# Branch A's attention with values as weights: the output comes out turned, and the division follows it

## The chip, the cores and the metric

The kernel runs on one core of a Trainium2 chip. The metric is the device time of one execution in microseconds (us). A core has a matrix engine (TensorE; PE for its matmuls and PEld for its weight loads in the profile), VectorE (DVE), ScalarE (ACT), GpSimd (POOL) and SyncE (SP), which issues most DMA transfers. Matmul results land in PSUM, in eight banks of 128 partitions by 512 f32; everything else works in SBUF.

## The reference

One layer of a bidirectional encoder, applied to a sample of 1024 tokens and a prompt of 256 tokens, 1024 channels wide, all in f32:

```python
h = _rmsnorm(x, g_mix)
z = h @ w_in                     # queries, keys, values of branches A and B, two gates
o_a, _ = _banded_attention(qa, ka, va, A_WINDOW, 1, rel_bias[:, :A_HEADS], sink)
o_b = _dilated_mixture(qb, kb, vb, rel_bias[:, A_HEADS:])
merged = gates[:, :, 0] * (o_a.reshape(b, S, A_Q) @ w_branch_a) + gates[:, :, 1] * (o_b @ w_branch_b)
x = x + merged @ w_out
h = _rmsnorm(x, g_mlp)
return x + jnp.square(jax.nn.relu(h @ w_up)) @ w_down
```

A final RMS norm follows. The change is in branch A: 8 query heads of 64 channels on 2 key and value heads, each query seeing the keys up to 128 tokens away, with a learned sink per head:

```python
p = jnp.exp(logits - m[..., None])
denom = jnp.sum(p, axis=-1) + jnp.exp(sink_r - m)
o = jnp.einsum('bngrqk,bnkgd->bnqgrd', p, vb)
o = o / denom[..., None]
```

## The kernel before

The 1280 tokens are ten tiles of 128 (tiles 0 to 7 are the sample, 8 and 9 the prompt). The program goes through stages: norm and values, the projections (with branch B's attention beside the last of them), branch A's attention, the gated branch outputs, the output projection, and the MLP. Most large products are made of three matmuls: each f32 operand is split into a high part (`hi`, a rounded copy made by ScalarE) and a low part (`lo`, the rest, subtracted by VectorE), and `mm3` (line 192) or `six` (line 351) multiplies low by high, high by low and high by high. Scores take two matmuls (lines 1071 and 1072). Probabilities and values are multiplied as plain f32, which the profile shows as two load and matmul passes for each matmul.

Branch A's attention runs head pair by head pair (`u`, 4 of them, two heads each) and tile by tile. A query tile sees its own key block of 128 and its neighbours: three blocks, or two at the ends of sample and prompt (tiles 0, 7, 8, 9). For one unit (head pair and tile), `scores` fills a bank for each head and VectorE adds the bias and takes the maximum; `exponential` is ScalarE's, and puts the row sums into `l_a`; `transposes` turns the probabilities on TensorE, and ScalarE (the first four blocks) and VectorE (the rest) move them to `pt`, whose slot `2 * b + h` holds block b of head h with keys on the partitions and queries in columns. `values_of` multiplies them into the one bank with tag "pv", VectorE copies the result to `o` (line 1111), and GpSimd writes it to the scratch tensor `scr_o[t]` (line 1112), a 128-column stripe for each head pair. The order on every engine is written out by hand here (a manual schedule): each turn of the loop handles two units, and between their steps it puts pieces of `logits`, the matmuls of five gate columns, and of `merge`, branch B's mixture, whose tiles `turn_merged` and `low_b` later turn and split.

After the last unit, `sums_a` adds the sink's share to `l_a` and takes the reciprocal. Then `load_o` (SyncE) brings back all heads of a tile, `divide` multiplies by the reciprocal sums on VectorE (line 1237), `turn_a` transposes the tile on TensorE (line 1246) and ScalarE writes its high part, and `low_a` makes the low part (line 1258). They run beside the 48 gated products ("jobs"): in a job TensorE multiplies a branch output of up to 512 tokens with 128 output columns, and VectorE multiplies the bank with the gate (lines 1385 and 1387) and adds for branch A (line 1388). The dictionary `side` says ahead of which job which step is issued; `load_gate` asks for a gate six jobs ahead (line 1332) and `open_gate` applies the sigmoid three jobs ahead (line 1337). The manual schedule ends before this loop; from there on a planner orders the instructions, in program order where it sees no reason against it, by costs it assumes.

Tiles of 4 KB for each partition come from one pool of 33 slots (`slot`). PSUM's banks are three "mm", two "sc", two "pt" and one "pv".

Of the kernel before, what the change touches and what calls it, by code (L numbers as in the profile page):

```python
# [13 lines left out]
ALU = mybir.AluOpType  # L14

P = 128
# [6 lines left out]
HD = 64  # L23
AH = 8
# [26 lines left out]
HALVES = (slice(0, HD), slice(HD, P))  # L51
# [46 lines left out]
def encoder_kernel(  # L98
# [5 lines left out]
    nc = tc.nc  # L104
# [22 lines left out]
    def slot(name, shape=(P, D), dt=F32):  # L127
        return slots.tile(list(shape), dt, name=name, tag="m", bufs=N_M)
# [7 lines left out]
    def bank(tag, name=None):  # L136
        return psum.tile([P, 512], F32, name=name or tag, tag=tag, bufs={"mm": 3, "sc": 2, "pt": 2, "pv": 1}[tag])
# [108 lines left out]
    ident = const.tile([P, P], F32, name="ident")  # L246
# [8 lines left out]
    l_a = const.tile([P, AH, NT], F32, name="l_a")  # L255
# [22 lines left out]
    scr_o = [dram.tile([P, AH * HD], F32, name=f"scr_o{t}") for t in range(NT)]  # L278
# [362 lines left out]
    with ExitStack() as pre:  # L641
# [166 lines left out]
        for t in range(2, NT):  # L808
# [13 lines left out]
            ps = bank("mm", "v")  # L822
# [18 lines left out]
        for t in (4, 5, 6, 7, 8, 9, 0, 1, 2, 3):  # L841
            ps = bank("mm", "v")
# [6 lines left out]
    if True:  # L849
# [177 lines left out]
        b, p = iter(()), parts0  # L1027
        att_b = iter(())
        for first, last, name in ((0, MIXED, "pairs"), (MIXED, len(PAIRS), "mixed")):
            with tc.tile_pool(name=name, bufs=1) as now[0]:  # L1030
                if first:
                    att_b = attention_b(stage)
                for j in range(first, last):
# [4 lines left out]
                    b, p = pair(b, p, PAIRS[j], PAIRS[j + 1] if j + 1 < len(PAIRS) else None, hooks, tick, first)  # L1038
# [10 lines left out]
    if True:  # L1049
# [7 lines left out]
        for t in range(NT):  # L1057
            s0, m = (0, 8) if t < 8 else (8, 2)
            lo, hi = max(t - 1, s0), min(t + 1, s0 + m - 1)
# [39 lines left out]
        def values_of(u, t):  # L1099
            lo, W, _ = tiles[t]  # L1100
            pt = live.pop((u, t))
            v, rest = units[u][0]["v"]
            pv = bank("pv")
            for h in range(2):
                for b in range(W // P):
                    k = lo + b
                    src = v[:, k, HALVES[u // 2]] if k < 8 else rest[:, k - 8, HALVES[u // 2]]
                    nc.tensor.matmul(pv[:, HD * h : HD * h + HD], pt[:, 2 * b + h, :], src,  # L1108
                                     start=b == 0, stop=b == W // P - 1)
            o = a3("o", (P, P), 3)  # L1110
            nc.vector.tensor_copy(o, pv[:, :P])
            nc.gpsimd.dma_start(scr_o[t][:, P * u : P * u + P], o)
# [88 lines left out]
    if True:  # L1201
        ob_hi, ob_lo = Wide("obhi", 2, F32R, ()), Wide("oblo", 2, F32R, ())
        o_hi, o_lo = Wide("ohi", 4, F32R, ()), Wide("olo", 4, F32R, ())
# [24 lines left out]
        rows_o = {}  # L1228

        def load_o(t):  # L1230
            rows_o[t] = slot("o", (P, AH, HD))
            nc.sync.dma_start(rows_o[t], scr_o[t].rearrange("p (h d) -> p h d", h=AH))

        def divide(t):

            o = rows_o[t]
            nc.vector.tensor_tensor(o, o, l_a[:, :, t].unsqueeze(2).to_broadcast([P, AH, HD]), op=ALU.mult)

        def turn_a(t):
            if t in (0, 4, 8):  # L1240
                o_hi.block(t // 4)
                o_lo.block(t // 4)
            o = rows_o.pop(t)
            ps = bank("pt")
            for k in range(4):
                nc.tensor.transpose(ps[:, P * k : P * k + P],
                                    o[:, 2 * k : 2 * k + 2, :].rearrange("p h d -> p (h d)"), ident)
            p3 = ps.rearrange("p (k q) -> p k q", k=4)
            per = o_hi.per(P * t)
            parts = [(o_hi.at(k, P * t, P, per), o_lo.at(k, P * t, P, per), p3[:, k : k + per, :])  # L1250
                     for k in range(0, 4, per)]
            banks_t["a", t] = parts
            for hi, _, src in parts:
                nc.scalar.activation(hi, src, AF.Copy)
# [14 lines left out]
        for j in range(0, n + 2, 2):  # L1269
# [31 lines left out]
            if j < n and order[j][1] == 0 and order[j][0] < 3:  # L1301
                u = order[j][0] + 1
# [40 lines left out]
        load_gate(3)  # L1343
        load_o(3)
        for i in range(4):
            divide(i)
            if i < 3:
                open_gate(i)
            next(fill)
        run(fill)  # L1350
        load_gate(4)
        load_gate(5)
        last.close()
        side = {0: [(turn_a, 0)], 1: [(low_a, 0), (turn_a, 1)], 2: [(low_a, 1), (turn_merged, 4)],
                3: [(low_b, 4), (turn_a, 2)], 4: [(low_a, 2), (turn_a, 3)], 5: [(low_a, 3), (turn_merged, 5)],
                6: [(low_b, 5), (turn_merged, 6)], 7: [(low_b, 6), (turn_merged, 7)], 8: [(low_b, 7), (divide, 4)],
                9: [(turn_a, 4), (divide, 5)], 10: [(low_a, 4), (turn_a, 5)], 11: [(low_a, 5), (divide, 6)],
                13: [(turn_a, 6)], 14: [(low_a, 6), (divide, 7)], 15: [(turn_a, 7)], 16: [(low_a, 7)],
                17: [(turn_merged, 8)], 18: [(low_b, 8), (turn_merged, 9)], 19: [(low_b, 9), (divide, 8)],
                20: [(turn_a, 8)], 21: [(low_a, 8), (divide, 9)], 22: [(turn_a, 9)], 23: [(low_a, 9)]}  # L1360
        for i, (x, b, c) in enumerate(jobs):
            t0, n = BLOCKS[b]
            load_gate(i + 6)
# [11 lines left out]
            hi, lo = w_bs[c // 4] if x == "b" else w_as[c // 2]  # L1375
            per, src = (4, (ob_hi, ob_lo)) if x == "b" else (2, (o_hi, o_lo))
            cols = slice(P * (c % per), P * (c % per) + P)
            ps = bank("mm")
# [76 lines left out]
    with ExitStack() as pre:  # L1455
# [20 lines left out]
        for hh in range(2):  # L1476
            sl = slice(512 * hh, 512 * hh + 512)
            ws = [weight(0) for _ in range(4)]
            parts = {}
# [16 lines left out]
            for t in range(NT):  # L1496
                m = parts.pop(t)
                ps = bank("mm")
# [246 lines left out]
    with ExitStack() as pre:  # L1745
# [106 lines left out]
        b = b0, p0  # L1852
        down = Down()
        last = FF // P // 2 - 1
        for j in range(last + 1):
            b = up(j, *b, entering() if not j else down.begin() if j == last else iter(()))
# [26 lines left out]
```

## Time and profile before

| | us |
|---|---|
| Median of three runs | 1737.16 (1736.12 to 1739.49) |
| Profiled execution | 1735.73 |
| Its span, first to last instruction | 1734.0 |

| Engine | Busy, us |
|---|---|
| TensorE matmuls | 1705.5 |
| TensorE weight loads | 1455.9 |
| VectorE | 976.3 |
| ScalarE | 727.0 |
| GpSimd | 520.7 |

The granted TensorE clock was 0.999 of full speed. Branch A's attention lies at about 560 to 719 us of the span, the division and the gated products at about 719 to 820 us. In lines of the profile, L1108 is line 1108 of the kernel; a row of instruction groups gives line, engine, operation, output and inputs, shapes (weights, then moving data, for a matmul), count, then busy time, mean duration in ns, idle time before and what ended it. A row of the timeline gives start, length, engine, line, operation and how many instructions in a row it merges. Matmuls are pipelined: a pass is listed for about 0.27 us or more, while the next one starts much earlier, so distances between starts are what a matmul costs.

### The profile page before, as it was taken

How to read it: one execution, taken by the hardware profiler on the slowest of the kernel's cores; microseconds unless marked ns; L12 is line 12 of the kernel's file. 1: busy time of each engine (PE TensorE's matmuls, PEld its weight loads, DVE VectorE, ACT ScalarE, POOL GpSimd, SP SyncE). 2: the span in 40 equal slices, each digit the busy share in tenths (PEclk: the TensorE clock that was granted, in tenths of full speed). 3: DMA queues.
4: the chain of work that ended last, by engine and by line, in shares of the span. 5: the costliest groups of instructions: out<-in, count | busy, mean ns of one | idle time of the engine just before them, and what ended most of it. 6: DMA issues, size and time to landing. Idle time of an engine off the chain costs nothing.

```text
span 1734.0 us, 25189 instructions
## 1 busy us (share of the span) xinstructions
PE 1705.5 (98%) x9248; PEld 1455.9 (84%) x9248; DVE 976.3 (56%) x1708; ACT 727.0 (42%) x1528; POOL 520.7 (30%) x452
## 2 busy tenths in 40 slices
PE   7999999999999999999999999999999999999998
PEld 6898888888888899888888788888888788888886
DVE  6732323455553566577558554545456876657575
ACT  6232223355552555555256334333334333333344
POOL 0212322212222344200100354645564442304050
PEclk9999999999999999999999999999999999999999
DMA  6414343576666743476112244334436844633333
GB/s 237 144 43 149 105 136 108 144 196 183 174 176 183 197 150 89 154 244 239 29 61 86 85 155 155 116 117 155 147 122 243 290 146 154 216 116 116 116 115 122
DMA packets 214779, 256.35 MB, mean 148 GB/s; under 512 B 24887, under 2 KB 144523, under 8 KB 214528
## 3 DMA queue, kind: packets, MB, share of 16 engines
q1 hardware_dynamic: 201424, 228.26, 40.8%
q0 software_dynamic: 12144, 24.38, 4.6%
q10 hardware_dynamic: 1088, 2.10, 0.3%
q8 instruction: 73, 1.20, 0.3%
q14 instruction: 50, 0.41, 0.1%
HBM read 169.10 MB, written 90.73 MB: 150 GB/s over the span
## 4 chain that ended last, share of the span: by engine, by line
PE 89%; DVE 4%; ACT 2%; DMA 2%; issue 2%; POOL 1%; SPq 0%; DVEq 0%; ACTq 0%; POOLq 0%
PE dn L351 21%; PE x L351 17%; PE mm L192 13%; PE z L351 9%; PE v L739 5%; PE pv L351 5%; PE mm L351 5%; PE y L351 4%; PE pv L1108 2%; PE pv L566 2%; PE sc L522 2%; PE pt L553 1%; PE pt L1095 1%; PE tr L342 1%; PE sc L1071 1%
## 5 line engine op out<-in xcount | busy, mean ns | idle before, releaser
L351 PE MATMUL dn<-dhi,ulo 128*128 128x512 f32 x448 | 174.6, 390 | 2.8 <-DVE ulo L186 2.8
L351 PE MATMUL dn<-dhi,uhi 128*128 128x512 f32 x448 | 174.3, 389 | 0.0
L351 PE MATMUL dn<-dlo,uhi 128*128 128x512 f32 x448 | 174.3, 389 | 0.0
L351 PE MATMUL x<-chi,wlo 128*128 128x512 f32 x424 | 167.5, 395 | 2.1 <-DVE u L1756 1.4
L351 PE MATMUL x<-clo,whi 128*128 128x512 f32 x424 | 165.7, 391 | 0.1
L351 PE MATMUL x<-chi,whi 128*128 128x512 f32 x424 | 165.1, 389 | 0.0
L318 DVE TENSOR_TENSOR wlo<-ta,whi 128x1024 fp32r<-128x1024 f32 x30 | 55.7, 1858 | 181.8 <-ACT whi L316 181.8
L318 DVE TENSOR_TENSOR wlo<-raw,whi 128x1024 fp32r<-128x1024 f32 x60 | 90.5, 1508 | 101.7 <-ACT whi L316 101.7
L393 POOL TENSOR_TENSOR tb<-raw 128x512 f32<-128x512 f32 x25 | 33.7, 1346 | 361.9 <-PE mm L192 137.4
L351 PEld LDWEIGHTS dn<-dhi,ulo 128*128 128x128 f32 x448 | 84.1, 188 | 21.1 <-DVE ulo L186 3.8
L186 DVE TENSOR_TENSOR ulo<-uraw,uhi 128x1024 fp32r<-128x1024 f32 x56 | 94.0, 1698 | 11.7 <-ACT uhi L185 11.7
L351 PEld LDWEIGHTS dn<-dhi,uhi 128*128 128x128 f32 x448 | 84.1, 188 | 17.7
L351 PEld LDWEIGHTS dn<-dlo,uhi 128*128 128x128 f32 x448 | 84.1, 188 | 17.3
L351 PEld LDWEIGHTS x<-chi,wlo 128*128 128x128 f32 x424 | 79.7, 188 | 20.4 <-issue 3.1
L351 PEld LDWEIGHTS x<-chi,whi 128*128 128x128 f32 x424 | 79.6, 188 | 17.1
L351 PEld LDWEIGHTS x<-clo,whi 128*128 128x128 f32 x424 | 79.8, 188 | 14.8 <-DVE clo L318 0.4
L1581 POOL TENSOR_TENSOR t<-raw,t 128x1024 f32<-128x1024 f32 x16 | 46.6, 2932 | 143.5 <-DMA raw<-in_w_down_dram 138.8
L1732 DVE TENSOR_TENSOR v<-v,dn 128x512 f32<-128x512 f32 x90 | 59.5, 681 | 43.2 <-PE dn L351 38.5
L1828 POOL TENSOR_TENSOR u<-u,u 128x640 f32<-128x640 f32 x16 | 25.6, 1597 | 162.8 <-ACT u L1753 162.8
L351 PE MATMUL pv<-phi,wlo 128*128 128x256 f32 x256 | 72.5, 283 | 1.7 <-ACT u L1752 1.7
L351 PE MATMUL dn<-dhi,up 128*128 128x512 f32 x224 | 73.5, 389 | 0.0
L543 ACT ACTIVATE s<-s,o 128x128 f32<-128x128 f32 (+1 forms) x120 | 51.9, 434 | 50.5 <-DVE o L535 46.5
(337 smaller groups left out, 4776.5 us busy)
## 6 DMA issues: line engine op xcount, KB each, us to landing
scr_u<-u SPq DMA_DIRECT2D x112, 320.0 KB, 2.6
uraw<-scr_u SPq DMA_DIRECT2D x56, 512.0 KB, 4.3
raw<-in_w_in_dram SPq DMA_DIRECT2D x33, 512.0 KB, 5.9
raw<-in_w_up_dram SPq DMA_DIRECT2D x32, 512.0 KB, 5.5
raw<-in_w_down_dram SPq DMA_DIRECT2D x28, 512.0 KB, 6.5
sg<-scr_g SPq DMA_DIRECT2D x32, 256.0 KB, 5.3
uraw<-scr_u SPq DMA_DIRECT2D x28, 256.0 KB, 4.3
v<-scr_v SPq DMA_DIRECT2D x96, 64.0 KB, 2.4
```

Of the source, the lines that this page charges most:

```text
L186: nc.vector.tensor_tensor(lo, src, hi.bitcast(F32), op=ALU.subtract)
L192: nc.tensor.matmul(ps, a, b, start=i == 0, stop=i == len(seq) - 1)
L318: nc.vector.tensor_tensor(lo, src, hi.bitcast(F32), op=ALU.subtract)
L351: nc.tensor.matmul(ps, a, b, start=first and i == 0, stop=last and i == len(seq) - 1, skip_group_check=True)
L393: (nc.vector if vector else nc.gpsimd).tensor_tensor(o, x, y, op=ALU.subtract)
L522: nc.tensor.matmul(at(k, h)[p0 : p0 + nq, :], qk[rows, p0 : p0 + nq], qk[rows, P + P * a : P + P * a + W], start=True, stop=True, skip_gro ...
L543: nc.scalar.activation(s[:, h, :W], s[:, h, :W], AF.Exp, bias=nm[:, h : h + 1], accum_out=l[:, h : h + 1])
L566: nc.tensor.matmul(pv[p0 : p0 + nq, HD * h : HD * h + HD], pt[:, 2 * k + h, p0 : p0 + nq], v[:, a + k, HALVES[h]], start=k == 0, stop=k == ...
L739: nc.tensor.matmul(ps[:, :n], a, b, start=k == 0 and j == 0, stop=k == KC - 1 and j == 2)
L1108: nc.tensor.matmul(pv[:, HD * h : HD * h + HD], pt[:, 2 * b + h, :], src, start=b == 0, stop=b == W // P - 1)
L1581: nc.gpsimd.tensor_tensor(o, a, b, op=ALU.subtract)
L1732: nc.vector.tensor_tensor(v, v, ps, op=ALU.add)
```

## The change

In `values_of` the operands change places. Before, the probabilities of a block (128 keys by 128 queries) are the weights and 64 columns of values move; a head's result has queries on the partitions and takes 64 columns of the bank. After, the 64 columns of values are the weights and 128 columns of probabilities move; a head's result has its 64 channels on one half of the partitions and 128 queries in columns, and both heads share the same 128 columns of the bank. The loop over blocks is now the outer one, so that the two heads alternate. The copy and the scratch write keep their shapes, and `scr_o[t]` now holds channels on partitions and queries in columns.

So the tile is already turned when it comes back, and the reciprocal sums, which lie with queries on the partitions, have to be turned instead. `divide` goes. A new step `widen` spreads the sums of two tiles over 64 channels each on GpSimd (two copies into a new slot); `turn_a` transposes the spread sums (again four transposes of 128 by 128), VectorE multiplies the loaded tile by them straight from the bank, and the high and low parts are then made from the product in SBUF instead of from the bank. The first two calls of `widen` stand where the first four calls of `divide` stood; the other three lie in `side`.

```diff
@@ values_of
-            for h in range(2):
-                for b in range(W // P):
-                    k = lo + b
-                    src = v[:, k, HALVES[u // 2]] if k < 8 else rest[:, k - 8, HALVES[u // 2]]
-                    nc.tensor.matmul(pv[:, HD * h : HD * h + HD], pt[:, 2 * b + h, :], src,
-                                     start=b == 0, stop=b == W // P - 1)
+            for b in range(W // P):
+                k = lo + b
+                src = v[:, k, HALVES[u // 2]] if k < 8 else rest[:, k - 8, HALVES[u // 2]]
+                for h in range(2):
+                    nc.tensor.matmul(pv[HALVES[h], :P], src, pt[:, 2 * b + h, :],
+                                     start=b == 0, stop=b == W // P - 1, skip_group_check=True)
@@ load_o, divide
-            rows_o[t] = slot("o", (P, AH, HD))
-            nc.sync.dma_start(rows_o[t], scr_o[t].rearrange("p (h d) -> p h d", h=AH))
-        def divide(t):
-            o = rows_o[t]
-            nc.vector.tensor_tensor(o, o, l_a[:, :, t].unsqueeze(2).to_broadcast([P, AH, HD]), op=ALU.mult)
+            rows_o[t] = slot("o", (P, 4, P))
+            nc.sync.dma_start(rows_o[t], scr_o[t].rearrange("p (u q) -> p u q", u=4))
+        wide_l = {}
+        def widen(t):
+            r = wide_l[t // 2] = slot("wl", (P, 2, AH, HD))
+            for i in range(2):
+                nc.gpsimd.tensor_copy(r[:, i], l_a[:, :, t + i].unsqueeze(2).to_broadcast([P, AH, HD]))
@@ turn_a
+            r = wide_l[t // 2][:, t % 2].rearrange("p h d -> p (h d)")
             for k in range(4):
-                nc.tensor.transpose(ps[:, P * k : P * k + P],
-                                    o[:, 2 * k : 2 * k + 2, :].rearrange("p h d -> p (h d)"), ident)
-            p3 = ps.rearrange("p (k q) -> p k q", k=4)
+                nc.tensor.transpose(ps[:, P * k : P * k + P], r[:, P * k : P * k + P], ident)
+            nc.vector.tensor_tensor(o, o, ps.rearrange("p (k q) -> p k q", k=4), op=ALU.mult)
             per = o_hi.per(P * t)
-            parts = [(o_hi.at(k, P * t, P, per), o_lo.at(k, P * t, P, per), p3[:, k : k + per, :])
+            parts = [(o_hi.at(k, P * t, P, per), o_lo.at(k, P * t, P, per), o[:, k : k + per, :])
@@ ahead of the gated products
-            divide(i)
+            if i < 2:
+                widen(2 * i)
@@ side: divide(4) to divide(9) go from jobs 8, 9, 11, 14, 19 and 21
+                3: [(low_b, 4), (turn_a, 2), (widen, 4)], ...
+                9: [(turn_a, 4), (widen, 6)], ...
+                13: [(turn_a, 6), (widen, 8)], ...
```

More of the change, by code (lines that the diff above doesn't have):

```diff
@@ L1354, in encoder_kernel @@
         side = {0: [(turn_a, 0)], 1: [(low_a, 0), (turn_a, 1)], 2: [(low_a, 1), (turn_merged, 4)],
[L1355 to L1360, printed above, removed]
+                3: [(low_b, 4), (turn_a, 2), (widen, 4)], 4: [(low_a, 2), (turn_a, 3)], 5: [(low_a, 3), (turn_merged, 5)],
+                6: [(low_b, 5), (turn_merged, 6)], 7: [(low_b, 6), (turn_merged, 7)], 8: [(low_b, 7)],
+                9: [(turn_a, 4), (widen, 6)], 10: [(low_a, 4), (turn_a, 5)], 11: [(low_a, 5)],
+                13: [(turn_a, 6), (widen, 8)], 14: [(low_a, 6)], 15: [(turn_a, 7)], 16: [(low_a, 7)],
+                17: [(turn_merged, 8)], 18: [(low_b, 8), (turn_merged, 9)], 19: [(low_b, 9)],
+                20: [(turn_a, 8)], 21: [(low_a, 8)], 22: [(turn_a, 9)], 23: [(low_a, 9)]}
         for i, (x, b, c) in enumerate(jobs):
```

## The prediction

> **What bounds the kernel now.** I read the page's busy shares and its chain that ended last, then the busy time by stretch around the lines that change, then the timeline inside that stage.
>
> ```profile
> span 1734.0 us, 25189 instructions
> PE 1705.5 (98%) x9248; PEld 1455.9 (84%) x9248; DVE 976.3 (56%) x1708; ACT 727.0 (42%) x1528; POOL 520.7 (30%) x452
> PE 89%; DVE 4%; ACT 2%; DMA 2%; issue 2%; POOL 1%; SPq 0%; DVEq 0%; ACTq 0%; POOLq 0%
> 580.00:719.00 139.00, 138.06 (x982) 127.55 (x982) 87.19 (x352) 74.35 (x209) 61.61 (x101) 1.00 0.45 128
> 730.00:760.00 30.00, 28.87 (x145) 23.56 (x143) 23.99 (x49) 19.93 (x44) 0.00 (x0) 1.00 0.94 330
> PE pt L1095 <- DVE pt L273: 0.8, 2, 0.4
> ```
>
> The rows of stretches give length, then busy time of PE, PEld, DVE, ACT, POOL, clock, DMA share. Branch A's attention (580 to 719) keeps TensorE busy for 138.06 of 139 us at clock 1.00, with DVE at 63% and ACT at 53%; the longest entry in TensorE's own waits there is 0.8 us in all. A TensorE microsecond saved here is a microsecond of the span, as long as nobody else becomes late. The division stage (730 to 760) is different: DVE is at 80% and DMA at 94%.
>
> **The change, part by part.** *Values.* There are 4 head pairs of 10 tiles; tiles 0, 7, 8 and 9 see two key blocks, the others three: 24 units of three blocks and 16 of two. Each block has one matmul for each of two heads, and each f32 matmul is two passes (a load and a move).
>
> ```profile
> L1108 PE MATMUL pv<-va,pt 128*128 128x64 f32 x352 | 43.3, 271 | 0.0
> L1108 PE MATMUL pv<-vp,pt 128*128 128x64 f32 x64 | 8.3, 273 | 0.1
> 586.76 1.45 PE L1108 MATMUL pv<-va,pt 128*128 128x64 f32 x12
> 588.05 0.83 PE L1095 MATMUL pt<-ident,s 128*128 128x128 f32 x6
> 588.71 1.45 PE L1108 MATMUL pv<-va,pt 128*128 128x64 f32 x12
> 589.97 0.37 PE L1071 MATMUL sc<-kp,qp 128*128 128x256 f32 x1
> 602.08 1.00 PE L1108 MATMUL pv<-va,pt 128*128 128x64 f32 x8
> 602.92 0.61 PE L1095 MATMUL pt<-ident,s 128*128 128x128 f32 x4
> 603.52 1.08 PE L1108 MATMUL pv<-vp,pt 128*128 128x64 f32 x8
> 604.40 0.42 PE L1071 MATMUL sc<-kk,q 128*128 128x384 f32 x1
> 604.66 0.34 PE L1072 MATMUL sc<-kk,q 128*128 128x384 f32 x1
> ```
>
> 352 + 64 = 416 passes = 24 x 12 + 16 x 8. Twelve take 1.29 us from start to the next instruction (586.76 to 588.05), eight 0.84 (602.08 to 602.92): about 0.107 each. A pass moves 64 columns behind a 128-column load. The transposes move 128 columns at the same pace (six from 588.05 to 588.71), so the load is what the values pay for. After a unit that ends on scores, the next matmul is late too (604.40 to 604.66 is 0.26, where 384 columns otherwise take 0.17). Counting that, a unit costs 1.32 us with three blocks and 0.87 with two.
>
> The changed form has 64 columns of weights, 128 columns moving, and the two heads in different halves of the output partitions. This trace has that shape, with 64 columns moving, in branch B's end tiles (L566), and 128 moving columns in L522's quarter-array matmuls:
>
> ```profile
> L566 PE MATMUL pv<-v,pt 128*64 128x64 f32 x96 | 5.4, 234 | 0.0
> 391.51 0.66 PE L566 MATMUL pv<-v,pt 128*128 128x64 f32 x9
> 391.71 0.28 PE L566 MATMUL pv<-v,pt 128*64 128x64 f32 x2
> 391.82 0.34 PE L566 MATMUL pv<-v,pt 128*64 128x64 f32 x6
> 392.09 0.33 PE L553 MATMUL pt<-ident,s 128*128 128x128 f32 x1
> L522 PE MATMUL sc<-qk x288: 269/320/480, 357.7 to 522.2; 64*128 64x128 f32 x48, 64*128 64x256 f32 x48, 64*64 64x128 f32 x48
> 393.53 0.45 PE L522 MATMUL sc<-qk 64*64 64x128 f32 x8
> 393.91 0.50 PE L351 MATMUL y<-hhi,wlo 128*128 128x512 f32 x1
> 394.25 0.40 PE L351 MATMUL y<-hlo,whi 128*128 128x512 f32 x1
> 394.48 0.39 PE L351 MATMUL y<-hhi,whi 128*128 128x512 f32 x1
> ```
>
> What to see: two passes start together at 391.71, and the other six, in 0.34 us with a pass of about 0.22, are three pairs 0.06 apart. So the two halves run side by side: eight passes take 0.45 us (5.4 / 12 groups). With 128 columns moving, eight passes on four tiles take 0.45 from 393.53; less the last one's 0.27 that is 0.16 to 0.17 between the first round and the second, a load of 0.05 that nothing hides and 0.107 of moving. Later rounds should come every 0.107 (128 columns), the 0.05 load being hidden: the 64-column rounds at 0.06 leave no room for a load and a move in turn.
>
> The price is the switch between whole array and halves. In: the last whole pass starts at 391.51, the first half pass 0.20 later instead of 0.107: 0.10. Out: from 393.69 to 393.91 is 0.21, and the next matmul runs with an unhidden load (393.91 to 394.25 is 0.34, then 0.23): 0.11; before transposes I take half of that, as their first one lasts 0.33 (392.09). The Trainium skill, "TensorEngine Tiling (Array Packing)", section Key Properties, says that changing the tiling mode drains TensorE; it speaks against this change, and these rows agree with a price of about 0.3 us for in and out.
>
> A unit after: 0.10 + 0.16 + (2n - 2) x 0.107 + 0.21 + 0.08, which is 0.98 us for n = 3 and 0.76 for n = 2. Saved: 24 x 0.34 + 16 x 0.11 = 8.2 + 1.8 = 10.0 us. Five of the two-block units now also enter late, as the second unit of an iteration waits until DVE has copied the only pv bank: four transposes from 602.92 would end at 603.36, the values start at 603.52 and their 0.88 includes an unhidden first load. The switch overlaps this wait: 5 x 0.2 = 1.0 more.
>
> ```profile
> L1111 DVE COPY o<-pv x40: 278/291/293, 573.2 to 719.4; 128x128 f32<-128x128 f32 x40
> ```
>
> That copy keeps its shape, and so does the scratch write behind it on POOL. From the last value pass its chain needs about 0.27 + 0.29 + two hops, some 0.75; TensorE's own way (out 0.21, four transposes with a late first one 0.39, in 0.20) takes 0.80, so it stays just covered; uncovered, it costs at most the 0.16 a unit that it costs now. The waits of TensorE on moved probabilities (0.8 us in all today) meet earlier arrivals; I take 0.5 back. Attention: 10.0 + 1.0 - 0.5 = 10.5 us.
>
> *Division.* Removed: ten DVE products (L1237, SBUF, four of them ahead of the gated loop). Added: ten DVE products of 128x512 that read PSUM, and ten POOL copies of 128x512. TensorE still does four transposes for each tile, now of the spread sums; they need POOL's copy and no longer the landing of o.
>
> ```profile
> L1237 DVE TENSOR_TENSOR o<-o,l_a 128x512 f32<-128x512 f32 x10 | 6.5, 683 | 2.5 <-DMA o<-scr_o 2.5
> L1385 DVE TENSOR_TENSOR mT<-mm,sg 128x512 f32<-128x512 f32 x16 | 10.7, 687 | 5.1 <-PE mm L192 5.1
> 736.47 0.69 DVE L1237 TENSOR_TENSOR o<-o,l_a 128x512 f32<-128x512 f32 x1 [2.46 <-DMA o<-scr_o]
> PE mm L192 <- DVE mT L1385: 1.1, 1, 1.1
> 741.66 0.75 DVE L1258 TENSOR_TENSOR olo<-pt,ohi 128x256 fp32r<-128x256 f32 x2
> 742.95 0.39 PE L192 MATMUL mm<-olo,whi 128*128 128x512 f32 x1
> L393 POOL TENSOR_TENSOR tb<-raw 128x512 f32<-128x512 f32 x25 | 33.7, 1346 | 361.9 <-PE mm L192 137.4
> L318 DVE TENSOR_TENSOR wlo<-ta,whi 128x1024 fp32r<-128x1024 f32 x30 | 55.7, 1858 | 181.8 <-ACT whi L316 181.8
> L235 DVE TENSOR_TENSOR wlo<-raw,whi 128x1024 fp32r<-128x1024 f32 x14 | 17.1, 1218 | 2.1 <-ACT whi L231 1.5 <-PE mm L192 0.4
> ```
>
> The DVE work is the same: a PSUM product takes 687 ns (L1385), an SBUF one 683. What changes is place. Today the product of tile 4 holds DVE for 2.46 us until o has landed, the gated products queue behind it, and TensorE loses 1.1 us for a bank. After, the product follows the transposes, later, when o has long landed: up to 1.1 won. Against it, the product lies inside the chain from transposes to the low part. Behind it on DVE wait the gated products, which free TensorE's banks, and on ACT the high part, with sigmoids and weight splits behind that. The tightest place is tile 3: its low part's first half is ready at about 742.05 and read at 742.95. A chain longer by 0.69 and a hop uses up that margin of 0.9, and four products that used to lie ahead of the loop (2.7 us) now lie in it, less the 2.46 of DVE waiting. The later tiles are turned well ahead of their use. I set the two against each other: 0, with bounds of 1.1 won and 2 lost.
>
> POOL's copy has no row. It has one input; the nearest row is a two-input POOL product at 1346 ns, so I take 1.3, at most 1.75, at least 0.6: 6 to 17 us on an engine that is idle here (POOL 0.00). Does it disturb DVE? The same DVE subtraction took 1858 ns in a group that shares its time with POOL and 1218 here. Bounds: 0, and a stretch by 1858 / 1218 = 1.53 over at most 15 us of copies, 5 us of DVE, against 30 - 23.99 = 6.0 of DVE's idle time: at most 3 us on TensorE. I take 0, as the change's own product and the gated products have an operand in PSUM and the copies have one input.
>
> The first two spreads (four copies) stand in POOL's queue behind the last scratch write, with nothing of this stage behind them. What hides them is the rest of the gate logits on TensorE; with that cover gone, the first transposes wait for one copy, 1.3 us.
>
> ```profile
> DMA to landing us min/median/max: 1.9/4.2/7.5
> ```
>
> Buffers: the spread sums take up to five of 33 slots, and o stays until its low part is made, so SyncE's gate loads (landing times above) run less far ahead. They are asked for six jobs before their product, which hides them, and I cost this at nothing; a gate that came late would cost up to one landing, 4.2 us.
>
> **Sum.** The profiled execution took 1735.73 us around a span of 1734.0; less 10.5 that is 1725.2. The median of the three runs, 1737.16, lies 1.43 above; on that footing the forecast is 1726.7 us.
>
> **Rivals.** *Loads do not hide.* If in halves each load waits for the move before it, each later round costs 0.16: (24 x 5 + 16 x 3) x 0.054 = 9.0 us are given back, leaving 1.5: 1735.7. For it: the first rounds do show 0.05 unhidden. Against: rounds 0.06 apart at 391.82. The Trainium skill, "TensorE: Matmul & The Clock Gate", Part 3, The mechanism, says loads overlap running matmuls only when the row group differs, and both heads use all rows here; by that rule this rival holds, and the trace so far disagrees.
>
> *The heads run one after the other.* Place: line 1108 in all 40 units. If 128 moving columns in each half can't be fed at once, a block has four rounds for two: (24 x 6 + 16 x 4) = 208 more rounds of 0.107 are 22.2 us, so 11.7 slower: 1748.9. It decides from the point where a pair of passes takes over 0.107 + 10.5 / 208 = 0.157 us. Against it: the pairs at 391.71 and the four tiles at 393.53; for it, no row has two heads with all 128 rows and 128 moving columns.
>
> *The division takes it back.* The upper bound above, 3 us in 730 to 760 through DVE: 1729.7. For it: DVE at 80% and a margin of 0.9. Against: DVE's idle 6.0 us and POOL's single input.
>
> **How the numbers follow.** Forecast 0.74, division 0.10, loads 0.07, heads in turn 0.09. About 0.2% (3.5 us) is what a measurement here can tell from no change, so faster means below 1733.7: 0.74 + 0.10 = 0.84; the loads rival is within it, 0.07; slower 0.09. The range goes from 1722.5 (1.1 won in the division, attention better by 1.5, and half the spread of the three runs) to 1731.5 (the division rival and the same spread).
>
> **What would show it.** Right: values with 128x64 weights, twelve or eight passes in 0.86 or 0.65 us of busy time with pairs together, the stage of attention about 10 us shorter, the same DVE and ACT busy time in it, no DVE wait on o at the gated loop's start, POOL copies near 1.3 us. Wrong: pairs 0.16 or 0.21 apart; switches of well over 0.3 us; new TensorE waits on the pv copy; TensorE idle by more than 3 us between the last values and the output projection.

## The result, and the profile after

The changed kernel takes 1728.67 us (median of four runs, 1727.62 to 1731.13) where the kernel before took 1736.7 (four runs). The ratio is 0.9953, with a 95% interval of 0.9935 to 0.997: 8.0 us faster. The forecast was 1726.7, in a range from 1722.5 to 1731.5. The profiled execution took 1728.73 us around a span of 1727.0, 7.0 less than before.

The page of the changed kernel, first its span and busy shares, then the shares of the chain that ended last:

```profile
span 1727.0 us, 25208 instructions
PE 1696.0 (98%) x9248; PEld 1432.4 (83%) x9248; DVE 978.5 (57%) x1708; ACT 727.4 (42%) x1528; POOL 525.7 (30%) x462
PE 85%; DVE 4%; issue 3%; ACT 2%; DMA 2%; POOL 2%; SPq 0%; ACTq 0%; POOLq 0%; DVEq 0%
```

The number of matmuls is the same, and TensorE is busy for 9.5 us less over the whole span. The span fell by 7.0 only, and TensorE's share of the chain went from 89% to 85%. Where it was won and lost is seen in stretches, so I cut both spans at the same four events: the first and the last pass of the values (L1108), the first gated product of branch B, and the last matmul of the gated products of branch A. Before (start and end, length, then busy time of PE, PEld, DVE, ACT and POOL, clock, DMA share, GB/s):

```profile
572.19:717.71 145.52, 144.54 (x1032) 133.54 (x1030) 91.08 (x366) 77.64 (x221) 66.42 (x109) 1.00 0.48 139
717.71:728.53 10.82, 10.82 (x64) 9.46 (x64) 8.30 (x19) 8.22 (x11) 0.54 (x1) 1.00 0.03 11
728.53:818.29 89.76, 88.63 (x481) 75.76 (x480) 63.46 (x115) 49.35 (x108) 0.00 (x0) 1.00 0.70 246
818.29:1733.96 915.67, 899.82 (x4355) 757.76 (x4353) 554.85 (x581) 356.80 (x618) 324.45 (x166) 1.00 0.41 137
```

After:

```profile
573.82:708.21 134.39, 132.49 (x1031) 109.68 (x1030) 91.06 (x366) 76.67 (x220) 66.17 (x109) 1.00 0.51 150
708.21:719.88 11.67, 11.11 (x67) 9.32 (x62) 6.86 (x16) 8.91 (x12) 3.87 (x6) 1.00 0.04 13
719.88:810.81 90.93, 89.30 (x480) 75.94 (x480) 65.37 (x118) 49.91 (x108) 4.00 (x7) 1.00 0.69 243
810.81:1726.96 916.15, 900.25 (x4355) 757.66 (x4353) 554.62 (x581) 356.85 (x618) 323.04 (x166) 1.00 0.41 137
```

| Stretch | Before, us | After, us | Change |
|---|---|---|---|
| up to the first value pass (same code) | 572.19 | 573.82 | +1.6 |
| attention, first to last value pass | 145.52 | 134.39 | -11.1 |
| last value pass to first gated product (the tail) | 10.82 | 11.67 | +0.85 |
| gated products to branch A's last (the loop) | 89.76 | 90.93 | +1.2 |
| the rest | 915.67 | 916.15 | +0.5 |

These sum to -7.0. The first row is scatter ahead of the change: a second profile of the changed kernel, below, has its first value pass at 572.28. The last row lies between 915.7 and 916.5 in all profiles below but one (920.4), with or without the change, so it is scatter too. What remains is 11.1 us won in attention, 0.85 lost in the tail and 1.2 lost in the loop.

The attention in detail. First the instructions of line 1108, then TensorE's timeline over two three-block units and two two-block units:

```profile
L1108 PEld LDWEIGHTS pv<-pt,va x352: 132/137/137, 573.8 to 703.5; 128*64 128x64 f32 x176
L1108 PE MATMUL pv<-pt,va x352: 272/273/324, 573.8 to 703.6; 128*64 128x128 f32 x176
```

```profile
586.75 0.82 PE L1095 MATMUL pt<-ident,s 128*128 128x128 f32 x6
587.50 0.88 PE L1108 MATMUL pv<-pt,va 128*64 128x128 f32 x12
588.31 0.88 PE L1095 MATMUL pt<-ident,s 128*128 128x128 f32 x6
589.11 0.88 PE L1108 MATMUL pv<-pt,va 128*64 128x128 f32 x12
589.92 0.38 PE L1071 MATMUL sc<-kp,qp 128*128 128x256 f32 x1
590.14 0.28 PE L1072 MATMUL sc<-kp,qp 128*128 128x256 f32 x1
...
601.27 0.66 PE L1108 MATMUL pv<-pt,va 128*64 128x128 f32 x8
601.86 0.66 PE L1095 MATMUL pt<-ident,s 128*128 128x128 f32 x4
602.45 0.66 PE L1108 MATMUL pv<-pt,vp 128*64 128x128 f32 x8
603.04 0.44 PE L1071 MATMUL sc<-kk,q 128*128 128x384 f32 x1
603.32 0.34 PE L1072 MATMUL sc<-kk,q 128*128 128x384 f32 x1
```

Twelve passes now take 0.81 us to the next instruction (587.50 to 588.31) where they took 1.29, eight take 0.59 (601.27 to 601.86) where they took 0.84. The two heads of a round start 6 to 7 ns apart, and the rounds of the unit at 589.11 follow one another after 0.160, 0.110, 0.109, 0.109 and 0.109 us: 0.05 us of loading shows ahead of the second round, the later loads are hidden. What the switch costs is seen around the values: six transposes between two units take 0.80 (588.31 to 589.11) where they took 0.66, and the first score matmul takes 0.22 (589.92 to 590.14) where others of its shape take 0.12.

The losses show in TensorE's waits behind the last values (708 to 760 us; waiting line, whom for, us in total, times, longest). The three longest:

```profile
PE pt L1250 <- DVE o L1251: 0.9, 1, 0.9
PE tm L1214 <- DVE o L1251: 0.6, 1, 0.6
PE mm L192 <- ACT gs L1133: 0.6, 1, 0.6
```

Before, this part had one wait, 1.1 us for the product that stood behind the late `o`. It is gone, and these have come. The third lies in the tail, ahead of the first gated product, and ends on ScalarE's copy of a gate's logits, which frees the bank. The first two lie in the loop and end on VectorE. VectorE's timeline, with idle time and its releaser in brackets:

```profile
707.38 0.29 DVE L1111 COPY o<-pv 128x128 f32<-128x128 f32 x1 [2.94 <-DMA scr_o<-o]
...
725.43 0.69 DVE L1251 TENSOR_TENSOR o<-o,pt 128x512 f32<-128x512 f32 x1 [2.75 <-DMA sg<-scr_g]
726.04 1.28 DVE L1389 TENSOR_TENSOR mT<-mm,sg 128x512 f32<-128x512 f32 x2
727.24 2.51 DVE L1261 TENSOR_TENSOR olo<-o,ohi 128x256 fp32r<-128x256 f32 x6
729.66 0.67 DVE L1251 TENSOR_TENSOR o<-o,pt 128x512 f32<-128x512 f32 x1
```

The copy at 707.38 waited 2.94 us for a scratch write to give back one of three `o` buffers (1.97 before, at 715.99). What stands behind it in VectorE's order comes later: the last values, the sums, and then ScalarE's work for the gates. In the loop the planner put the products of tiles 0, 1 and 2 ahead of the first gated product on VectorE. The third, at 725.43, has an idle 2.75 us in front of it although both gated products behind it (726.04) had their banks by then. The label names a gate's DMA; the transposes that this product reads started at 724.79, and in the repeat of this kernel the same idle time is put down to them. This is a case where the releaser named is not the one that decided.

### The profile page after: what moved, and what is told of

Read it like the earlier page. It is cut to its first block, busy times and chain, and to the rows that moved or that the text cites. A ratio compares the mean times of both kernels' runs of the same rounds, so it can differ in the third digit from the quotient of the medians.

```text
span 1727.0 us, 25208 instructions
## 1 busy us (share of the span) xinstructions
PE 1696.0 (98%) x9248; PEld 1432.4 (83%) x9248; DVE 978.5 (57%) x1708; ACT 727.4 (42%) x1528; POOL 525.7 (30%) x462
## 4 chain that ended last, share of the span: by engine, by line
PE 85%; DVE 4%; issue 3%; ACT 2%; DMA 2%; POOL 2%; SPq 0%; ACTq 0%; POOLq 0%; DVEq 0%
PE dn L351 21%; PE x L351 18%; PE mm L192 11%; PE z L351 9%; PE v L739 6%; PE pv L351 5%; PE mm L351 5%; PE y L351 4%; PE pv L566 2%; PE sc L522 1%; PE pt L553 1%; PE tr L342 1%; PE pv L1108 1%; PE pt L1095 1%; DVE clo L318 1%
```

## The experiments

The texts on record speak of theories by letters where there are several. For the loop, the last of these questions, theory C says that only the planner's order of the steps costs time there, and theory D that the longer chain of a tile (transposes, product, high part, low part) costs it in any order.

**The change again.** A second measurement with five runs, on the chip of the next three experiments.

> The changed kernel again, timed beside the parts below. In the two profiles it was 7.0 us shorter by span, of which 1.5 us more passed before branch A's attention had begun, in code that is the same in both. If that 1.5 us is run to run scatter, five rounds give 8 to 9 us less than before (1727.5 to 1729); if it belongs to the change, 7 us less.

Measured: 1727.99 us (1727.61 to 1728.37), ratio 0.9947 [0.9934, 0.9959], span 1726.6. Attention took 135.19, with one wait of 1.0 us on moved probabilities at the stage's start that the first profile doesn't have; the tail 11.67, the loop 90.95. So the gains and losses of the table repeat, and the time falls into the 8 to 9 us of the first alternative.

**Values alone and division alone.** The first keeps the new `values_of` with the old `divide` and `turn_a`; the second keeps the old `values_of` with the new division.

```diff
 e1: values_of as after; load_o, divide, turn_a and side as before
 e2: values_of as before; load_o, widen, turn_a and side as after
```

> Values as weights, but the division as before (it divides and turns the tile as if it still lay with queries on the partitions, so the output is not the reference's). Theory A, that the values save about 10.5 us and the new division loses about 2: 9.5 to 11 us less than before, 1726 to 1727, and faster than the whole change by 1.5 to 2.5. Theory B, that the division costs nothing and the values themselves are worth only 8: the same time as the whole change, 1728 to 1729.

> The new division with the old values (probabilities as weights; the output is not the reference's, as the tile does not lie turned). Theory A: 1.5 to 2.5 us slower than before, 1738 to 1739.5, with VectorE idle ahead of the third product. Theory B: the same as before within 0.5 us.

Measured: values alone 1727.65 us (1726.38 to 1729.12), ratio 0.9944 [0.993, 0.9957]; division alone 1737.85 (11 runs), ratio 1.0005 [0.9996, 1.0013]. The whole gain is that of the values. Theory A was missed in size: values alone are 0.3 us faster than the repeat of the change, not 1.5 to 2.5, and 9.1 faster than before, not 9.5 to 11. (The profiled execution of values alone, the slowest of its five, spent 3.4 us of the attention at half clock, a scatter that the last section comes back to.) The division by itself can't be told from no change by its time, so by time its cost isn't shown. Its profile shows the place: its loop, 730.09 to 820.87, took 90.78 us (89.76 before), with the same waits in the loop as after:

```profile
PE pt L1250 <- DVE o L1251: 0.9, 1, 0.9
...
PE tm L1214 <- DVE o L1251: 0.6, 1, 0.6
```

Its tail took 10.83, as before, while the tail of values alone took 11.68. So the loss in the tail belongs to the values. In the loop the division lost 1.0 us beside the old values, but only 0.55 beside the new ones (90.93 less 90.38): values alone already lost 0.6 there. The old wait on the product of tile 4 was 1.2 us there for 1.1, and the rest is in TensorE's busy time (89.14 us for 88.63), spread thinly; I can't attribute it.

**The heads in turn.** The same instructions with the two loops exchanged, so that all passes of one head stand ahead of those of the other.

```diff
-            for b in range(W // P):
-                ...
-                for h in range(2):
+            for h in range(2):
+                for b in range(W // P):
```

> The change with the loop over heads outside and blocks inside, so that the passes of one head come after those of the other. If the gain comes from two halves of the array working at once, the pairs go: up to 22 us slower than the change, 1745 to 1751, twelve-pass units of about 1.4 us instead of 0.8. If the gain came from the lighter weight load, or if the array takes the other half's passes out of turn, it stays at 1728 to 1730.

Measured: 1733.73 us (10 runs), ratio 0.9984 [0.9975, 0.9993], 5.7 slower than the change: between the two forecasts. TensorE's timeline of this kernel:

```profile
587.55 1.15 PE L1108 MATMUL pv<-pt,va 128*64 128x128 f32 x12
588.63 0.87 PE L1095 MATMUL pt<-ident,s 128*128 128x128 f32 x6
...
676.50 0.66 PE L1095 MATMUL pt<-ident,s 128*128 128x128 f32 x4
677.09 0.67 PE L1108 MATMUL pv<-pt,vp 128*64 128x128 f32 x8
677.68 0.45 PE L1071 MATMUL sc<-kk,q 128*128 128x384 f32 x1
```

Eight passes take 0.59 as before the exchange, twelve take 1.08 in place of 0.81. Though the program has the heads in turn, the second head's passes start beside the first head's: with two blocks right from the first round (13 ns apart), with three from the third (589.705 beside 589.700). The profile doesn't name the head of a pass; I read it off the rhythm and off the length of a half's first pass, 0.32 us for 0.27. In both cases a pass starts beside the one that stands four places ahead of it in the program. 24 three-block units at 0.27 are 6.5 us, near the 5.7 measured. That the heads overlap without alternating is shown by this run.

**Six buffers for the turned-back output.** Against the tail's wait: `o` gets six buffers in place of three, paid for by moving half of the bias loads to other slots.

```diff
-            o = a3("o", (P, P), 3)
+            o = a3("o", (P, P), 6)
...
-                units[u] = load_unit(u), load_bias(u, lambda name, shape: a3(name, shape, 2))
+                units[u] = load_unit(u), load_bias(u, (lambda name, shape: a3(name, shape, 1)) if u % 2 else wslot)
```

> The change with six buffers instead of three for the copied head outputs (the room comes from one bias buffer, which goes to a weight slot). At the end of the attention VectorE waited 2.9 us for a scratch write to free one. Theory E, that this wait sets the end of the attention: that wait gone, 0.7 to 1.5 us faster than the change (1726.5 to 1727.3). Rival: the chain of table loads, sums and reciprocals behind the last unit ends last anyway: no change within 0.4 us.

Measured: 1726.91 us (1724.93 to 1728.88), ratio 0.9938 [0.9925, 0.995], span 1724.2. VectorE's copy now waits 0.84 us for values only, and TensorE's stretches of attention and tail:

```profile
572.89:706.45 133.56, 132.31 (x1030) 109.69 (x1030) 91.10 (x367) 77.89 (x222) 66.44 (x109) 1.00 0.54 152
706.45:717.31 10.86, 10.86 (x66) 9.31 (x63) 6.28 (x15) 8.28 (x11) 4.26 (x6) 1.00 0.02 7
```

The tail is back at its length of before, and the wait of 0.53 us at the last values is gone. So in the planner's order the wait for the three buffers made the tail longer. It isn't the only way to get the time back: the hand order below keeps three buffers and a copy that waits 2.71 us for them, and its tail is 10.85 us. There ScalarE loads a function table (1.28 us each) once in the tail, not three times, as the sigmoid that the planner puts ahead of the sums' exponential stands behind it. In time six buffers are 1.1 us by the medians; the intervals of this and the change overlap, so the profile carries this verdict.

**The loop by hand.** The manual schedule ends behind the loop, or at its job 5, in place of ahead of it, so that the order written in the program holds on every engine.

```diff
-        last.close()                       # ahead of the loop
+        last.close()                       # e4: behind the loop
+            if i == 5:
+                last.close()               # e8: in the loop
```

> The change with the hand-written order kept through the gated loop, so that VectorE's products of the spread sums stand where the program has them, between the gated products, and not three in a row ahead of the first gated product. Theory C, that the planner's order costs the 1.0 to 1.4 us that the loop lost: 1.0 to 1.5 us faster than the change (1726.5 to 1727) and no TensorE wait on the product of line 1251. Theory D, that the longer chain from transposes to low part costs it in any order: the same as the change, or slower by up to 2 us, as the hand order also takes away the early gate loads.

> The change with the hand-written order kept through the first five gated jobs only, and the planner from the sixth on; the full hand order was stopped at job five by a weight split. Theory C, that the three products ahead of the first gated product cost the loop its 1.0 to 1.4 us and more (TensorE waits of 1.0, 0.7 and 0.3 us there): those three waits gone, 1.0 to 2.0 us faster than the change, 1726 to 1727. Theory D, that the longer chain costs it in any order: the waits come back at another place, within 0.5 us of the change.

Measured: 1731.31 us, ratio 0.9963 [0.995, 0.9975], and 1730.42, ratio 0.995 [0.9936, 0.9964]. Neither is better than the change; by the ratios the second can't be told from it. The three waits are gone, and one takes their place, in the first (TensorE's timeline, then the stretches behind it):

```profile
729.79 0.40 PE L192 MATMUL mm<-obhi,whi 128*128 128x512 f32 x1
733.62 0.66 PE L1214 MATMUL tm<-ident,merged 128*128 128x128 f32 x2 [3.43 <-DVE oblo L1226]
...
734.50 0.63 PE L192 MATMUL mm<-oblo,whi 128*128 128x512 f32 x1
734.93 0.63 PE L192 MATMUL mm<-obhi,whi 128*128 128x512 f32 x1
```

```profile
733.50:739.00 5.50, 5.38 (x14) 4.35 (x15) 3.09 (x7) 2.61 (x5) 1.17 (x2) 0.50 1.05 386
739.00:745.00 6.00, 6.00 (x30) 4.92 (x30) 2.97 (x6) 1.34 (x3) 0.00 (x0) 0.97 0.32 118
```

The wait of 3.43 us would already eat the gain. Behind it the clock was granted at 0.50 for the next 5.5 us, with matmuls 0.43 us apart in place of 0.23. The hand order to job 5 has 3.3 us at the same place. What ended these waits is not the division alone. In the first, VectorE stood idle for 2.01 us ahead of a weight split (line 235) that needed ScalarE's part of it; ScalarE had itself waited 1.6 us for a product of line 1251 just before. In the second, ScalarE's timeline shows a gate that came late:

```profile
724.91 0.72 ACT L1340 ACTIVATE sg<-sg,bg 128x512 f32<-128x512 f32 x1
730.77 0.72 ACT L1340 ACTIVATE sg<-sg,bg 128x512 f32<-128x512 f32 x1 [5.14 <-DMA sg<-scr_g]
```

The gate landed at 730.75; the high part of a tile, its low part and the product that TensorE waited for all stood behind its sigmoid. So neither forecast came true (theory D allowed 2 us and 0.5 us of loss), and the two runs don't decide between theories C and D: the order by hand brings waits of its own, and no run has the old division in that order.

**The product one job later.** A third order, by the planner again: the product leaves `turn_a` and gets a job of its own, the low part one job behind that.

```diff
-            nc.vector.tensor_tensor(o, o, ps..., op=ALU.mult)      # in turn_a
+        def product_a(t): ...                                      # one job later
-        side = {0: [(turn_a, 0)], 1: [(low_a, 0), (turn_a, 1)], ...
+        side = {0: [(turn_a, 0)], 1: [(product_a, 0), (turn_a, 1)], 2: [(low_a, 0), (product_a, 1), ...
```

> The whole change, with the product by the turned sums (line 1251) taken out of `turn_a` into a step of its own, one job behind the transposes, and the low part one job behind that, so that no step of the division waits in the same job for the step ahead of it. The planner still orders the instructions, and it still puts three products ahead of the first gated product on VectorE, but the low parts of the first three tiles now stand between and behind the gated products. Theory C (the places that the planner gave the steps cause the loss in the loop): the three waits of TensorE (0.9, 0.6 and 0.6 us) shrink to under 1 us together, first to first gated product of branches B and A goes from 15.6 to 14.2 to 14.7 us, and the kernel is 0.9 to 1.4 us faster than the change alone, 1726.6 to 1727.1. Theory D (the product makes the chain of a tile longer and costs it in any order): the waits move to the low parts that come later, the distance stays at 15.3 or more, and the time is within 0.7 us of the change's.

Measured: 1728.59 us, ratio 0.9953 [0.9939, 0.9967]: as the change. Its profiled execution was the slowest of five (1734.91), most of it lost in the MLP, so I read only the loop: 91.23 us, first to first gated product of the two branches 15.7 (15.6 in the change), and these two waits in it:

```profile
PE mm L192 <- DVE mT L1397: 1.1, 1, 1.1
PE pt L1250 <- DVE o L1257: 0.9, 1, 0.9
```

The wait on the transposes of merged tiles (0.6) is gone, and one of 1.1 on a gated product has come, as theory D has it. That speaks for theory D. It isn't proof: three products still stand ahead of the first gated product in this order, and the two orders by hand lost their time at other places.

**Pairs of units.** If the switch between whole array and halves is the rest of the price, fewer switches should save it: the values of two units are issued together, into two 128-column stripes of the "pv" bank, 20 pairs of switches in place of 40. For room and order the run also has three `pt` buffers for two, the bias loads of the six buffers, and the values one turn later.

```diff
-        def values_of(u, t):
+        def values_of(*pair):
+            for n, (u, t) in enumerate(pair):
...
-                    nc.tensor.matmul(pv[HALVES[h], :P], src, pt[:, 2 * b + h, :],
+                        nc.tensor.matmul(pv[HALVES[h], P * n : P * n + P], src, pt[:, 2 * b + h, :],
...
-                values_of(*order[j - 3])
+                values_of(order[j - 4], order[j - 3])
```

> The change with the values of two units issued together, into two column ranges of the one bank, one turn later: 20 switches into halves and out instead of 40. By the rows each costs 0.31 to 0.36 us (0.10 in, 0.05 first load, 0.10 out, 0.05 to 0.11 next load): 6 to 7 us faster than the change, 1721 to 1722. Rival: the switch is cheap and what was counted as its price is waiting that only moves (banks, moved probabilities): less than 2 us faster.

Measured: 1723.71 us (1722.54 to 1725.75), ratio 0.9922 [0.991, 0.9935], 4.3 faster than the change where 6 to 7 were expected. TensorE's timeline in the stage and at its end:

```profile
592.80 1.53 PE L1109 MATMUL pv<-pt,va 128*64 128x128 f32 x24
594.26 0.66 PE L1095 MATMUL pt<-ident,s 128*128 128x128 f32 x4
...
702.62 1.09 PE L1109 MATMUL pv<-pt,vp 128*64 128x128 f32 x16 [1.58 <-DVE mm__7486 L1167]
```

Twenty-four passes take 1.46 us where two times twelve took 1.62, and a pair saves one entry and one exit besides. Most of what is missing is at the end: the last pair waits 1.58 us, behind a copy that waits 3.24 us for the three buffers. The third `pt` buffer and the moved loads were not run by themselves.

**Pairs with a free buffer at the end, and pairs by hand.** In the first the last tiles' outputs go to a buffer of scores that is free by then. The other two are pairs with the loop by hand (all of it, and to job 5 with the free buffer).

```diff
-                o = a3("o", (P, P), 3)
+                o = a3("s", n=4)[:, 0, :P] if u == 3 and t > 5 else a3("o", (P, P), 3)
```

> The pairs, with the head outputs of the last four units copied into score buffers that are free by then instead of the three output buffers, one of which the last pair had to wait for (1.7 us of TensorE). That wait gone: 1.2 to 1.8 us faster than the pairs, 1722 to 1722.5, and 6 us faster than the change, as the switches alone would give. Rival: the chain of sums behind the last pair takes it back: the same as the pairs, 1723.7.

> The pairs and the hand-written order through the gated loop together. If both theories hold, the gains add: 1720 to 1721. If the loop's loss is not the planner's, the same as the pairs alone.

> The pairs with the late outputs in score buffers and the hand-written order through the first five gated jobs. If the gains add, 1720.5 to 1721.5; under theory D the same as the pairs with late outputs.

Measured: 1722.7 us (1720.88 to 1724.84), ratio 0.9905 [0.9888, 0.9921]; 1725.77, ratio 0.9935 [0.9921, 0.9948]; 1723.8, ratio 0.9914 [0.9901, 0.9928]. The pairs with a free buffer have the lowest median, below both kernels of this case. Against the pairs alone the intervals overlap; the profile shows the wait at the last values gone and a tail of 10.85. Two of their four runs took 1720.9 and 1721.1 us, the others 1724.3 and 1724.8. The profiled one is the slowest, and it has a pause of TensorE of 3.11 us at the stage's start and half clock behind it, which the pairs alone don't have. Order by hand gains nothing here either, and the gains don't add: the wait of 3.4 us at the merged tiles is there in the second, one of 2.6 in the third, again behind a gate that came late (ScalarE idle for 4.4 us).

## Why the prediction was right, and where it was not

*Values: right, term by term.* Forecast for a unit with its switches: 0.98 and 0.76 us. From the rows above, two three-block units cost 0.81 + 0.81, 0.09 for the transposes ahead (0.75 for 0.66), 0.14 for those between and 0.10 for the late score: 0.98 each. Two two-block units cost 0.59 + 0.59, some 0.09 ahead, 0.15 between (0.59, where four transposes alone take 0.44) and 0.11 late: 0.77. So the 10.0 us of the sum were there, and attention as a whole came out 10.3 to 11.1 shorter for 10.5 forecast. The rounds follow one another after 0.109 us (0.107 forecast), the second after 0.160 (0.16). The terms for entries and waits (1.0 and 0.5) were not measured by themselves.

*"Loads do not hide": fell.* The rounds at 0.109 leave no room for a load of 0.05 that waits. The Trainium skill's rule, on which this rival drew ("TensorE: Matmul & The Clock Gate", Part 3, The mechanism: loads overlap running matmuls only when the row group differs), is not what this trace shows. Here both heads use the same rows and different columns, and the later loads are hidden. The section's own words ahead of that rule also let a load into the background weight buffer go first, which this result doesn't contradict.

*"The heads run one after the other": fell,* and so clearly that even heads in turn in the program cost 5.7 us where the rival had 22.2.

*The tail: a term that the sum lacked.* The prediction said that the copy "keeps its shape, and so does the scratch write behind it", and costed the copy's own chain at 0.75 us against 0.80 of TensorE's way. It did not ask what faster units do to the buffers of that copy: the scratch writes take no less time than before (2.5 us at the median from issue to landing, 2.0 before), and the three buffers come free too late at the end. That is 0.85 us in the planner's order; six buffers take it away.

*Division: taken as 0, measured as +0.55 to +1.0 us in the loop* (beside the new and the old values; 1.2 for the whole change). The step that failed is "I set the two against each other". Both sides of it happened: the wait of 1.1 us for the late `o` is gone, and in its place the first products wait for transposes, ahead of the gated products that free TensorE's banks. The new waits in the loop (0.9, 0.6 and 0.2 us) are 0.5 us more than the one removed. The rest is 0.67 us more of TensorE's busy time in the loop (89.30 for 88.63), of which values alone have 0.5; its cause stays open, and so does whether another order would win the waits back. The bounds held it (1.1 won to 2 lost). The lengths were right: the product takes 678 ns, near the 687 of its row.

*POOL's copy: mis-sized, on the safe side, and its disturbance not zero.* The instructions of lines 1240 and 1261 after (minimum, median and maximum in ns), and POOL's timeline:

```profile
L1240 POOL COPY wl<-l_a x10: 608/614/1585, 716.8 to 736.2; 128x512 f32<-128x512 f32 x10
L1261 DVE TENSOR_TENSOR olo<-o,ohi x18: 410/418/832, 727.2 to 768.0; 128x256 fp32r<-128x256 f32 x16, 128x512 fp32r<-128x512 f32 x2
728.72 1.50 POOL L1240 COPY wl<-l_a 128x512 f32<-128x512 f32 x2 [7.51 <-DVE olo L1261]
```

The copy takes 0.61 us, the lower bound, not 1.3. And one low part took 832 ns for 418: the one at 728.9, beside POOL's copies from 728.72, which took 0.75 and 0.80 themselves. The copy of 1585 ns started at 716.84, 0.1 us after a weight split on VectorE (line 235, 1.23 us) that also reads two tiles in SBUF. The prediction argued that the change's own product and the gated products read PSUM, and overlooked that the change also turned the low part into an operation with two inputs from SBUF. It is 0.4 us on VectorE, just ahead of the product that ends TensorE's wait of 0.6, so up to 0.4 us of that wait may be its work; no run took the copies away to show it. The Trainium skill, "SBUF — State Buffer", section "SBUF: two separate sides", says that VectorE with two SBUF inputs and GpSimd reading SBUF share a port pair by an exclusive lock; a delay of 414 ns beside copies of 608 agrees with it.

*The sum.* 10.5 forecast, less 0.85 and 1.2, are 8.45 us; 8.0 and 8.8 were measured. The mechanism of the gain was right; the two losses were not in the sum, and that the time stayed inside the range is owed in part to room that was left for another loss. The rival "The division takes it back" was nearest in time (1729.7), for another reason than its own: it wanted 3 us lost through VectorE beside POOL's copies, and the loop lost 1.2. Slots and gate loads cost TensorE nothing in the changed kernel, as costed: no wait of TensorE on them is listed, though ScalarE waited 2.5 us for one gate.

## What to carry to other kernels

A small matmul that uses half of the array's columns pays for itself when a partner for the other half stands within about four passes of it, and when each switch between whole array and halves is shared by many passes. Here a switch in and out cost about 0.3 us by the rows (0.09 in, 0.05 for the first load, 0.09 out, 0.05 to 0.10 on the next load), and 0.2 to 0.3 by the time that twenty fewer of them saved. When a stage gets faster, ask for each buffer that it gives away when it comes back: the transfers here took no less time than before. A step that moves into a chain can cost time although its engine has no more work, so name the queue that it will stand in, not only the engine that has time for it. And a run that changes the order of steps changes every wait in that order: see which wait ends last before it is taken as a test of one step.

## What the runs showed of the hardware

Three things I had not expected. TensorE starts a pass of one column half beside a pass of the other half that stands four places ahead of it in the program: head 2's first of six at 589.705, beside head 1's third at 589.700.

The clock was granted at 0.50 for stretches of about 3.4 us or twice that behind some pauses of TensorE, and the length of the pause alone doesn't say which. In values alone a pause of 1.23 us was enough; in the pairs with a free buffer by hand to job 5 one of 2.59 us was not (stretches around both; the third row is the second run's):

```profile
578.30:581.70 3.40, 1.76 (x19) 1.23 (x18) 2.87 (x8) 2.63 (x8) 1.04 (x2) 1.00 0.74 223
581.70:585.10 3.40, 3.40 (x19) 2.89 (x18) 1.91 (x10) 1.19 (x5) 1.15 (x2) 0.50 0.10 32
726.20:729.60 3.40, 2.36 (x12) 1.99 (x13) 3.40 (x8) 3.40 (x10) 0.00 (x0) 1.00 1.07 373
```

Pauses of 3.11, 3.33 and 3.43 us were followed by half clock too (in the hand order to job 5 only 1.4 us after the pause had ended), with matmuls 0.43 us apart in place of 0.23. I can't give a rule from these rows. The Trainium skill, "TensorE: Matmul & The Clock Gate", Part 1, What's actually happening, names an idle window of about 3.4 us and a half rate; the half rate agrees, and the stretch at half clock has that length, but the pause of 1.23 us shows that TensorE need not be idle for so long.

And beside a one-input copy on GpSimd, a VectorE operation that has two inputs in SBUF took 832 ns for 418; it did so in the repeat of the change and in the division alone as well.
